# Weighing the values in float32r parts in the first layer's attention, and a beat of three steps for one kind of head

## The chip, the cores and the metric

The kernel runs on one core of a Trainium2 chip. The metric is the device time of one execution in microseconds (us), taken as the median of several runs of one kernel. A profiled execution gives the trace; its own time stands beside its span below.

TensorE is called PE in the profile (PEld: its loads of the stationary operand), VectorE DVE, ScalarE ACT, GpSimd POOL, SyncE SP.

## The reference

A decoder trunk of two layers over 256 positions and 2048 channels. The first layer's attention has two kinds of heads; this case is about the product of softmax weights and values in both.

```python
def even_mixer(x, w_in, sinks, w_out):
    h = jnp.einsum('bsd,de->bse', x, w_in)
    # kind A: 16 query heads on 2 key/value heads, window 128, a learned sink per head, ALiBi
    oa, _ = banded_attention(qa, ka, va, A_WINDOW - 1, 1, ...)
    # kind B: 8 heads, three dilations (1, 4, 16), merged by their denominators
    for gi, (window, dil) in enumerate(B_PATTERNS):
        o, lse = banded_attention(to_strided(qb, dil), to_strided(kb, dil), to_strided(vb, dil), ...)
    mix = jax.nn.softmax(jnp.stack(lses), axis=0)
    ...
    return jnp.einsum('bse,ed->bsd', y, w_out)      # y: A's 16 heads, then B's 8

def reference(x, ...):
    for layer in range(DEPTH):
        x = layer_norm(ALPHA * x + mixer(x), ...)
        x = layer_norm(ALPHA * x + sqrelu_mlp(x, ...), ...)
```

All is float32. The second layer has other mixers, and the code of their attention stays as it is.

## The kernel before, in words

**Dense products.** All weights come from memory once, in units of 512 KB (128 partitions of 1024 floats). SP's queue loads a unit into a `raw` tile; ACT casts it to float32r (`w_hi`, line 120); DVE subtracts and keeps the rest, also as float32r (`w_lo`, line 121). A dense product is hi times hi, lo times hi and hi times lo, each one pass of the array in float32r. `ws` (lines 329 and 332) has the weights as the stationary operand and streams x (512 columns with both parts of x, 256 with its high part); `as_` (lines 379 to 381) has x or y as the stationary operand and streams the weights, 512 columns at a time. Splits run three units ahead of PE, loads five.

**Attention.** It is cut into steps that are laid between the units of the dense work: after each unit the loop calls `pump`, and that calls `attn_step` once. The order is fixed by the program; each engine works through its own queue in that order. A `Job` holds one kind of heads, taken in pairs. A started pair computes scores (`qk`, line 699, float32), bias and maxima on DVE, exponentials on ACT one or two steps on, the division on DVE after that. `lag` steps later each head's weights are turned by three PE transposes into the one PSUM tile `pt`, and ACT copies them to an SBUF tile `pT` (`flip`, lines 260 and 262), one flip a step. Two steps after the flip of the odd head of a pair, `weigh` multiplies the pair's `pT` with the values. Jobs: A has 16 heads and starts a pair every second step (`pace=2`); B0 and B1 have 4 heads with three dilations each (`per=3`), which add up in one PSUM tile `o`.

In `weigh` the values are stationary, 128 keys by 64 columns, so the two heads of a pair stand side by side in the array; the `pT` stream is 256 columns for the first block of keys and 128 for the second, all in float32 (lines 279 and 281), which PE runs as two instructions for each product. After the last one ACT casts `o` to a float32r `y` and DVE subtracts its rest (lines 285 and 286).

So there are 8 weighings for A and 12 for B, 20 in all. The last of B1 come in `finish`, without dense work between the steps: the third column block of the output projection calls it when it needs B1's result, two units before its end.

**The names used below.** W is one weighing, F one flip's three transposes, S the scores of one pair (two heads). The tile pools are rings: `S` 4, `pT` 4, `qk` 15, `xfull` 2, `o` 1, `pt` 1, `sc` 2, `acc` 4.

Of the kernel before, what the change touches and what calls it, by code (L numbers as in the profile page):

```python
# [30 lines left out]
HD = 64  # L31
# [35 lines left out]
class Stream:  # L67


    def __init__(self, k):  # L70
        self.k = k
        self.units = []
        self.nd = 0
        self.ns = 0
        self.nu = 0
        self.live = {}
# [74 lines left out]
class Job:  # L151


    def __init__(self, name, n, per, score, stages, value, lag, y, pace=2):
        self.name, self.n, self.per, self.lag, self.pace = name, n, per, lag, pace
        self.score, self.stages, self.value, self.y = score, stages, value, y
        self.left = n // 2
        self.out = []
        self.s = {}
        self.pt = {}  # L160
        self.o = None


class Trunk:
# [48 lines left out]
    def attn_step(self):  # L213
        i = self.i
        self.i += 1
        if self.flips and self.flips[0][0] <= i:
            _, job, h, u = self.flips.popleft()
            self.at_step(i, 2, self.flip, job, h, u)
            if h % 2:
                self.at_step(i + 2, 1, self.weigh, job, (h - 1, h), u)  # L220
        for _, _, fn, args in sorted(self.due.pop(i, []), key=lambda t: t[:2]):
            fn(*args)
        if not self.todo or i < self.turn:
            return
        job, h, u = self.todo[0]
        per, pair = job.per, (h, h + 1)
        if h not in job.s:
            need = 2 if per > 1 else 1
            if self.s_live + need > self.s_bufs:
                return  # L230
            self.s_live += need
            if per > 1:
                for g in pair:
                    job.s[g] = self.at.tile([P, per * 384], F32, name="S", bufs=self.s_bufs)
            else:
                both = self.at.tile([P, 768], F32, name="S", bufs=self.s_bufs)
# [17 lines left out]
    def flip(self, job, h, u):  # L254

        nc = self.nc
        st = job.s[h]
        pt = self.ps.tile([P, 384], F32, name="pt")
        for b in range(3):
            nc.tensor.transpose(pt[:, b * P:(b + 1) * P], st[:, u * 384 + b * P:u * 384 + (b + 1) * P], self.ident)  # L260
        pT = self.at.tile([P, 384], F32, name="pT", bufs=self.pt_bufs)
        nc.scalar.copy(pT, pt)
        job.pt[(h, u)] = pT
        if u == job.per - 1 and (job.per > 1 or h % 2):
            self.s_live -= 1

    def weigh(self, job, heads, u):
        nc = self.nc
        first, last = u == 0, u == job.per - 1
        if first and heads[0] % 2 == 0:  # L270
            job.o = self.ps.tile([P, S], F32, name="o")
        o = job.o
        for blk in range(2):
            for h in heads:
                rows = slice((h % 2) * HD, (h % 2) * HD + HD)
                w = job.pt[(h, u)]
                v = job.value(h, u, blk)
                if blk == 0:
                    nc.tensor.matmul(o[rows, :], v, w[:, 0:S], start=first, stop=False, skip_group_check=True)  # L279
                else:  # L280
                    nc.tensor.matmul(o[rows, P:S], v, w[:, S:S + P], start=False, stop=last, skip_group_check=True)
        if last and heads[-1] % 2:
            y = job.y(len(job.out))
            yh, yl, _ = y
            nc.scalar.copy(yh, o)
            nc.vector.tensor_tensor(yl, o, yh.bitcast(F32), op=ALU.subtract)
            job.out.append(y)
            job.left -= 1

    def y_at(self, k=None):  # L290
        return self.parts(self.at.tile([P, 2 * S], F32R, name="y", bufs=self.y_bufs))

    def parts(self, t):
        return t[:, 0:S], t[:, S:2 * S], t
# [149 lines left out]
    def setup(self):  # L444
        nc, a, const = self.nc, self.a, self.const
        nc.scalar.preload_act_table_set("natural_log_exp_and_others")
        zeros = self.at.tile([P, 512], BF16, name="zeros")
        nc.vector.memset(zeros, 0.0)
        self.keep_clock(IDLE[0], zeros)
        self.ident = const.tile([P, P], F32, name="ident")  # L450
        nc.sync.dma_start(self.ident, a["ident"])
        self.x = self.res.tile([P, 2, D], F32, name="x_res")
        xv = a["x"][0].rearrange("(t p) d -> p t d", p=P)
        for c0, c1, ahead in ((0, 256, 1), (256, 512, 2), (512, 1024, 4), (1024, 1536, 5), (1536, 2048, 6)):
            nc.sync.dma_start(self.x[:, :, c0:c1], xv[:, :, c0:c1])
            self.w._dma(ahead)
        gb = self.at.tile([16, 8, P], F32, name="gb")
        rg = self.at.tile([6, P], F32, name="rg")
        self.sinks = const.tile([P, 16], F32, name="sinks")
        self.masks = self.at.tile([P, 4, 384], F32, name="masks")  # L460
        small = [(gb[:, i * 2:i * 2 + 2, :], a[nm].rearrange("l (k p) -> k l p", p=P))
                 for i, nm in enumerate(("ln1_g", "ln1_b", "ln2_g", "ln2_b"))]
        small += [(rg[0:4, :], a["odd_q_norm_g"][0].rearrange("(k p) -> k p", p=P)),
                  (rg[4:6, :], a["odd_kv_norm_g"][0].rearrange("(k p) -> k p", p=P)),
                  (self.masks, a["m_even"]), (self.sinks, a["even_sinks"][0].unsqueeze(0).to_broadcast([P, 16]))]

        def load(some):
            for dst, src in some:
                nc.gpsimd.dma_start(dst, src)

# [276 lines left out]
    def even(self):  # L747
        nc = self.nc
        slopes = alibi(16)
        qa = self.project(512, scale=0.125) + self.project(512, scale=0.125)  # L750
        kd = self.tile2()
        va = self.tile2()
        kvf = self.at.tile([P, 2, S], F32, name="kvf", bufs=1)
        vf = kvf[:, 1, :]

        def take(f, bank):
# [10 lines left out]
        def flip_v():  # L767
            pt = self.ps.tile([P, 384], F32, name="pt")
            for t in range(2):
                nc.tensor.transpose(pt[:, t * P:(t + 1) * P], vf[:, t * P:(t + 1) * P], self.ident)  # L770
            nc.vector.tensor_copy(va[:, :, 0:P], pt[:, 0:S].rearrange("p (t c) -> p t c", t=2))

        self.at_step(self.i, 0, flip_v)
        top, power, divide = self.softmax(1, sink=lambda h: self.sinks[:, h:h + 1])
# [6 lines left out]
            nc.vector.scalar_tensor_tensor(st, self.masks[:, 0, :], -slopes[h], sc, op0=ALU.mult, op1=ALU.add)  # L781
            top(h, st)

        def value(h, u, blk):
            return va[:, blk, (h // 8) * HD:(h // 8) * HD + HD]

        self.vb = []
        ja = Job("A", 16, 1, score, (bias, power, divide), value, 5, self.y_at)
        self.queue(ja)
        jb = [self.even_b(0, self.y_at), self.even_b(1, self.x_slot)]  # L790
        self.finish(jb[0])
# [10 lines left out]
        for c in range(3):  # L802
            o = self.as_(late if c == 2 else ys, 12 if c == 2 else 10, 512)
            self.add_res(o, c, True, st if c == 2 else None)
            self.pump()
        for c in range(2):
            o = self.as_(jb[1].out, 2, 512)
# [4 lines left out]
    def even_b(self, half, y):  # L812
        nc = self.nc
        sl = alibi(8)
        qkv = []
# [9 lines left out]
            if u == 2:  # L825
                top(h, st)

        def value(h, u, blk):
            return qkv[u][2][:, blk, h * HD:h * HD + HD]

        job = Job(f"B{half}", 4, 3, score, (bias, power, divide), value, 4, y)
        for gi in range(3):
            q = self.project(256, scale=0.125)[0]
            k = self.project(256)[0]
# [296 lines left out]
    def go(self):  # L1131
        tc = self.tc
        self.plan()
        for layer in range(2):
            if layer == 0:
                self.s_bufs, self.pt_bufs, self.qk_bufs, self.y_bufs = 4, 4, {"qk": 15}, 10
            else:
                self.s_bufs, self.pt_bufs, self.qk_bufs, self.y_bufs = 4, 4, {"c": 8, "d": 10}, 14
            with tc.tile_pool(name=f"at{layer}", bufs=1) as self.at:
# [44 lines left out]
```

## Time and profile before

| | |
|---|---|
| median of 3 runs | 2182.63 us (2182.18 to 2182.82) |
| profiled execution, own time | 2183.56 us |
| its span | 2181.8 us |
| PE busy / DVE busy / ACT busy | 2161.2 / 1392.9 / 1063.9 us |
| granted TensorE clock | 0.999 |
| first layer's attention in the span | about 85 to 370 us |
| 85 to 135 us: DVE busy, ACT busy | 44.77, 35.09 of 50 us |

How to read it: the share of busy time says that PE is nearly always at work, but matmuls are pipelined and their ends are modelled, so what one piece of work is worth is read from the distance of ends in the chain of work that ended last. The chain's rows are "start, length, what"; a piece ends where the next begins. In the timelines and groups a row's length is that of the whole instruction, which overlaps its neighbours.

### The profile page before, as it was taken

What the parts mean: (1) busy time and instruction counts of PE and PEld (TensorE: products, weight loads), DVE (VectorE), ACT (ScalarE), POOL (GpSimd) and SP (SyncE); (2) the same over time, 40 slices, a digit from 0 to 9 for tenths busy, and PEclk for the clock granted to TensorE, in tenths of its full rate; (3) what the DMA queues carried; (4) which work ended last, traced back from release to release, by engine and by line L of the source; (5) the groups of instructions that cost most, each with busy time, mean ns of one, the idle gap of its engine ahead of it and who ended that gap; (6) DMA issues with size and microseconds to landing.
All of it is one profiled execution on the core that took longest, in us unless ns stands there. A gap on an engine that the chain in (4) does not pass through costs nothing.

```text
span 2181.8 us, 29446 instructions
## 1 busy us (share of the span) xinstructions
PE 2161.2 (99%) x11324; PEld 1816.7 (83%) x11324; DVE 1392.9 (64%) x1912; ACT 1063.9 (49%) x1532; POOL 34.4 (2%) x64
## 2 busy tenths in 40 slices
PE   9999999999999999999999999999999999999998
PEld 7878887888888888888878787778888888888886
DVE  5765566775465556456568888878645655554656
ACT  4554544554354355345345667545534534543542
POOL 0000000000000000000012000000000000000000
PEclk9999999999999999999999999999999999999999
DMA  7545554565656665656558554466665656556553
GB/s 265 157 136 174 158 166 149 189 201 193 192 180 203 193 188 190 194 175 205 190 155 210 167 150 145 155 193 204 206 193 179 198 197 192 185 194 192 186 197 119
DMA packets 222269, 399.02 MB, mean 183 GB/s; under 512 B 12778, under 2 KB 52416, under 8 KB 221360
## 3 DMA queue, kind: packets, MB, share of 16 engines
q1 hardware_dynamic: 219424, 386.78, 56.2%
q0 software_dynamic: 2416, 9.84, 1.9%
q8 instruction: 88, 1.44, 0.3%
q10 hardware_dynamic: 288, 0.52, 0.1%
q14 instruction: 53, 0.43, 0.1%
HBM read 395.00 MB, written 2.10 MB: 182 GB/s over the span
## 4 chain that ended last, share of the span: by engine, by line
PE 94%; issue 2%; DMA 1%; DVE 1%; ACT 1%; POOL 1%; SPq 0%; POOLq 0%; ACTq 0%; DVEq 0%
PE acc L332 18%; PE acc L379 15%; PE acc L380 15%; PE acc L381 15%; PE acc L329 9%; PE sc L332 5%; PE sc L329 3%; PE pt L332 3%; PE o L332 3%; PE sc L699 2%; PE o L329 1%; PE pt L329 1%; PE pt L260 1%; PE o L279 1%; PE acc L985 1%
## 5 line engine op out<-in xcount | busy, mean ns | idle before, releaser
L121 DVE TENSOR_TENSOR w_lo<-raw,w_hi 128x1024 fp32r<-128x1024 f32 (+3 forms) x748 | 883.6, 1197 | 605.2 <-ACT w_hi L120 601.2
L120 ACT CAST w_hi<-raw 128x1024 fp32r<-128x1024 f32 (+3 forms) x748 | 760.3, 1030 | 733.1 <-PE acc L381 440.2
L332 PE MATMUL acc<-x,w_hi 128*128 128x512 f32 x1824 | 453.7, 394 | 4.3 <-DVE x L520 4.1
L379 PE MATMUL acc<-w_hi,h_hi 128*128 128x512 f32 x1016 | 395.3, 389 | 0.0
L380 PE MATMUL acc<-w_lo,h_hi 128*128 128x512 f32 x1016 | 395.3, 389 | 0.0
L381 PE MATMUL acc<-w_hi,h_lo 128*128 128x512 f32 x1016 | 395.2, 389 | 0.0
L332 PEld LDWEIGHTS acc<-x,w_hi 128*128 128x128 f32 x1824 | 330.9, 189 | 68.1 <-issue 2.9
L329 PEld LDWEIGHTS acc<-x,w_lo 128*128 128x128 f32 x1824 | 244.1, 191 | 17.9 <-issue 3.8
L329 PE MATMUL acc<-x,w_lo 128*128 128x256 f32 x1824 | 254.4, 284 | 0.0
L381 PEld LDWEIGHTS acc<-w_hi,h_lo 128*128 128x128 f32 x1016 | 190.7, 188 | 39.6
L379 PEld LDWEIGHTS acc<-w_hi,h_hi 128*128 128x128 f32 x1016 | 190.7, 188 | 39.4
L380 PEld LDWEIGHTS acc<-w_lo,h_hi 128*128 128x128 f32 x1016 | 190.7, 188 | 39.3
L332 PE MATMUL sc<-x,w_hi 128*128 128x512 f32 x512 | 138.7, 392 | 0.0
L379 PE MATMUL acc<-w_hi,x 128*128 128x512 f32 (+1 forms) x304 | 119.5, 393 | 0.3 <-DVE x L519 0.2
L381 PE MATMUL acc<-w_hi,x 128*128 128x512 f32 (+1 forms) x304 | 115.8, 381 | 0.0
L380 PE MATMUL acc<-w_lo,x 128*128 128x512 f32 (+1 forms) x304 | 115.7, 381 | 0.0
L345 ACT ACTIVATE xfull<-acc 128x256 f32<-128x256 f32 x130 | 49.5, 383 | 128.5 <-PE acc L332 77.6
L332 PEld LDWEIGHTS sc<-x,w_hi 128*128 128x128 f32 x512 | 91.0, 189 | 14.6
L329 PE MATMUL sc<-x,w_lo 128*128 128x256 f32 x512 | 84.3, 282 | 0.0
L329 PEld LDWEIGHTS sc<-x,w_lo 128*128 128x128 f32 x512 | 76.6, 190 | 6.4
L332 PE MATMUL pt<-x,w_hi 128*128 128x512 f32 x256 | 79.3, 391 | 0.0
L332 PE MATMUL o<-x,w_hi 128*128 128x512 f32 x256 | 78.9, 389 | 0.0
(208 smaller groups left out, 1954.5 us busy)
## 6 DMA issues: line engine op xcount, KB each, us to landing
raw<-in_mlp_w SPq DMA_DIRECT2D x512, 512.0 KB, 4.1
raw<-in_even_w_in SPq DMA_DIRECT2D x92, 512.0 KB, 4.1
raw<-in_odd_w_in SPq DMA_DIRECT2D x56, 512.0 KB, 4.5
raw<-in_odd_w_out SPq DMA_DIRECT2D x32, 512.0 KB, 3.7
raw<-in_even_w_out SPq DMA_DIRECT2D x24, 512.0 KB, 3.9
gb_rows<-in_ln_g POOLq DMA_DIRECT2D x3, 1024.0 KB, 5.1
gb_rows<-in_ln_b POOLq DMA_DIRECT2D x3, 1024.0 KB, 7.1
raw<-in_odd_w_uq SPq DMA_DIRECT2D x8, 384.0 KB, 4.7
```

What stands on the lines that cost most here:

```text
L120: nc.scalar.copy(h, r)
L121: nc.vector.tensor_tensor(l, r, h.bitcast(F32), op=ALU.subtract)
L260: nc.tensor.transpose(pt[:, b * P:(b + 1) * P], st[:, u * 384 + b * P:u * 384 + (b + 1) * P], self.ident)
L279: nc.tensor.matmul(o[rows, :], v, w[:, 0:S], start=first, stop=False, skip_group_check=True)
L329: nc.tensor.matmul(banks[f][:, S:2 * S], lo[:, c:c + P], xs[kt + kk][0], start=False, stop=wide and kt + kk == nkt - 1, skip_group_check=True)
L332: nc.tensor.matmul(banks[f], hi[:, c:c + P], xs[kt + kk][2], start=kt + kk == 0, stop=not wide and kt + kk == nkt - 1, skip_group_check=True)
L345: nc.scalar.activation(t, bank[:, S:2 * S], AF.Copy, scale=scale)
L379: nc.tensor.matmul(outs[t], xh[:, ts], hi[:, c:c + width], start=first, stop=False, skip_group_check=True)
L380: nc.tensor.matmul(outs[t], xh[:, ts], lo[:, c:c + width], start=False, stop=False, skip_group_check=True)
L381: nc.tensor.matmul(outs[t], xl[:, ts], hi[:, c:c + width], start=False, stop=last, skip_group_check=True)
L699: nc.tensor.matmul(sc[:, cols], q[:, qs], k[:, ks], start=True, stop=True, skip_group_check=True)
L985: nc.tensor.matmul(banks[h], hi[:, c:c + P], both, start=k == 0, stop=False, skip_group_check=True)
```

## The change

For both kinds of heads in the first layer, the weighing is done with float32r parts.

- `flip` makes two tiles: ACT casts `pt` to a float32r `pT`, then DVE subtracts and writes the rest to `pL`. Both read the PSUM tile `pt`. `pT` and `pL` have three buffers each (before: `pT` four).
- The values are split as well (`split_values`): for each key block and head 128 columns hold the high part (64) and the low part (64). A does this once (`va`); B does it for every pair and dilation one step before the weighing (`value_parts`, tile `vp`, two buffers), by an ACT cast and a DVE subtraction.
- `weigh_parts`: for each head and key block the 128 columns are stationary, and `pT`, then `pL` are streamed: 8 matmuls for a pair, four of 256 columns and four of 128. The two heads have a column range of `o` each (now 512 columns). The output rows of high and low values lie in the two halves of the partitions; after the last matmul two ACT copies and two DVE additions bring them together in an `xfull` tile, and the cast and the subtraction to `y` follow from there.
- A starts a pair every third step (`pace=3`).
- For room: `zeros` uses a buffer of `pT`, the gains (`gb`, `rg`) use a buffer of `S`, `kvf` comes from the `qk` ring, and `va` has a shape of its own in it.

```diff
@@ attn_step
-                self.at_step(i + 2, 1, self.weigh, job, (h - 1, h), u)
+                if job.parts:
+                    self.at_step(i + 1, 4, self.value_parts, job, h - 1, u)
+                self.at_step(i + 2, 1, self.weigh_parts if job.parts else self.weigh, job, (h - 1, h), u)
@@ flip
+            hi = self.at.tile([P, 384], F32R, name="pT", bufs=self.pt_bufs)
+            lo = self.at.tile([P, 384], F32R, name="pL", bufs=self.pt_bufs)
+            nc.scalar.copy(hi, pt)
+            nc.vector.tensor_tensor(lo, pt, hi.bitcast(F32), op=ALU.subtract)
+            job.pt[(h, u)] = hi, lo
@@ new
+    def split_values(self, dst, src):
+        self.nc.scalar.copy(dst[:, :, :, 0, :], src)
+        self.nc.vector.tensor_tensor(dst[:, :, :, 1, :], src, dst[:, :, :, 0, :].bitcast(F32), op=ALU.subtract)
+
+    def weigh_parts(self, job, heads, u):
...
+        for j, h in enumerate(heads):
+            for blk, cols, ws in ((0, slice(j * S, j * S + S), slice(0, S)), (1, slice(j * S + P, j * S + S), slice(S, S + P))):
+                stat = v(j, blk)
+                for n, w in enumerate(job.pt[(h, u)]):
+                    nc.tensor.matmul(o[:, cols], stat, w[:, ws], start=first and j + blk + n == 0,
+                                     stop=last and blk == 1 and n == 1, skip_group_check=True)
...
+        nc.scalar.copy(other[lo], o[hi, 0:S])
+        nc.scalar.copy(other[hi], o[lo, S:2 * S])
+        nc.vector.tensor_tensor(full[lo], o[lo, 0:S], other[lo], op=ALU.add)
+        nc.vector.tensor_tensor(full[hi], o[hi, S:2 * S], other[hi], op=ALU.add)
...
+        nc.scalar.copy(yh, full)
+        nc.vector.tensor_tensor(yl, full, yh.bitcast(F32), op=ALU.subtract)
@@ even
-        ja = Job("A", 16, 1, score, (bias, power, divide), value, 5, self.y_at)
+        ja = Job("A", 16, 1, score, (bias, power, divide), None, 5, self.y_at, pace=3, parts=parts)
@@ even_b
+        def parts(h, u):
+            v = self.at.tile([P, 2, 2, 2, HD], F32R, name="vp", bufs=2)
+            self.split_values(v, qkv[u][2][:, :, h * HD:(h + 2) * HD].rearrange("p t (h e) -> p t h e", h=2))
+            return lambda j, blk: v[:, blk, j].rearrange("p a e -> p (a e)")
-        job = Job(f"B{half}", 4, 3, score, (bias, power, divide), value, 4, y)
+        job = Job(f"B{half}", 4, 3, score, (bias, power, divide), None, 4, y, parts=parts)
@@ go
-                self.s_bufs, self.pt_bufs, self.qk_bufs, self.y_bufs = 4, 4, {"qk": 15}, 10
+                self.s_bufs, self.pt_bufs, self.qk_bufs, self.y_bufs = 4, 3, {"qk": 15}, 10
```

**How the order moves.** PE, a pair of A during an `as_` product: `acc` rows are dense work, `o` is W, `pt` F, `sc` S. Before:

```order
L279 MATMUL o<-pT,qk 64x256 x2
L281 MATMUL o<-pT,qk 64x128 x2
L260 MATMUL pt<-ident,S 128x128 x3
L699 MATMUL sc<-qk 128x128 x2
L699 MATMUL sc<-qk 128x256 x2
L379 MATMUL acc<-w_hi,x_143 128x512
L380 MATMUL acc<-w_lo,x_143 128x512
```

The same place in the changed kernel (`pL` is the low part of the weights; `qk` is here `va`):

```order
L322 MATMUL o<-pT,qk 128x256
L322 MATMUL o<-pL,qk 128x256
L322 MATMUL o<-pT,qk 128x128
L322 MATMUL o<-pL,qk 128x128
L322 MATMUL o<-pT,qk 128x256
L322 MATMUL o<-pL,qk 128x256
L322 MATMUL o<-pT,qk 128x128
L322 MATMUL o<-pL,qk 128x128
L264 MATMUL pt<-ident,S 128x128 x3
L429 MATMUL acc<-w_hi,x_142 128x512
L430 MATMUL acc<-w_lo,x_142 128x512
```

W has eight rows of its own, and S no longer stands right behind W and F: it comes a unit later, behind the pair's other flip.

DVE at the same place, from one pair's `y` on. Before (`dn`, `rc` and `S<-S,rc` are a head's division, `S<-masks,sc` with `mx` and `nm` a head's bias and maximum):

```order
L286 TENSOR_TENSOR y<-o,y 128x256
L735 TENSOR_TENSOR dn<-dn,es 128x2
L737 RECIPROCAL rc<-dn 128x2
L739 TENSOR_SCALAR S<-S,rc 128x128
L739 TENSOR_SCALAR S<-S,rc 128x256
L781 SCALAR_TENSOR_TENSOR S<-masks,sc 128x384
L713 TENSOR_REDUCE mx<-S 128x1 x2
L716 TENSOR_SCALAR nm<-mx,sinks 128x2
L781 SCALAR_TENSOR_TENSOR S<-masks,sc 128x384
```

Now:

```order
L331 TENSOR_TENSOR xfull<-o,xfull 64x256
L332 TENSOR_TENSOR xfull<-o,xfull 64x256
L336 TENSOR_TENSOR y<-xfull,y 128x256
L269 TENSOR_TENSOR pL<-pt,pT 128x384
L785 TENSOR_TENSOR dn<-dn,es 128x2
L787 RECIPROCAL rc<-dn 128x2
L789 TENSOR_SCALAR S<-S,rc 128x128
L789 TENSOR_SCALAR S<-S,rc 128x256
L121 TENSOR_TENSOR w_lo<-raw,w_hi 128x1024
L269 TENSOR_TENSOR pL<-pt,pT 128x384
```

Two additions and a `pL` are new behind the weighing, and the second flip's `pL` stands behind a weight split (`w_lo`); a pair has three steps, so three `w_lo` in place of two.

PE at the end of B1, where no dense work lies between the steps. Before:

```order
L260 MATMUL pt_3463<-ident_88,S_2716 128x128 x3
L260 MATMUL pt_3475<-ident_88,S_2715 128x128 x3
L279 MATMUL o_3458<-pT_3438,vb_1923 64x256
L279 MATMUL o_3458<-pT_3467,vb_1923 64x256
L281 MATMUL o_3458<-pT_3438,vb_1923 64x128
L281 MATMUL o_3458<-pT_3467,vb_1923 64x128
L260 MATMUL pt_3485<-ident_88,S_2716 128x128 x3
L279 MATMUL o_3458<-pT_3479,vb_2351 64x256
```

Now (the values come from `vp`):

```order
L264 MATMUL pt_3694<-ident_88,S_2896 128x128 x3
L264 MATMUL pt_3708<-ident_88,S_2895 128x128 x3
L322 MATMUL o_3685<-pT_3660,vp_3716 128x256
L322 MATMUL o_3685<-pL_3661,vp_3716 128x256
L322 MATMUL o_3685<-pT_3660,vp_3716 128x128
L322 MATMUL o_3685<-pL_3661,vp_3716 128x128
L322 MATMUL o_3685<-pT_3698,vp_3716 128x256
L322 MATMUL o_3685<-pL_3699,vp_3716 128x256
L322 MATMUL o_3685<-pT_3698,vp_3716 128x128
L322 MATMUL o_3685<-pL_3699,vp_3716 128x128
L264 MATMUL pt_3727<-ident_88,S_2896 128x128 x3
L322 MATMUL o_3685<-pT_3712,vp_3735 128x256
```

The sequence of F and W is the same. DVE in that stretch, before:

```order
L121 TENSOR_TENSOR w_lo_3417<-raw_3280,w_hi_3416 128x1024
L121 TENSOR_TENSOR w_lo_3441<-raw_3309,w_hi_3440 128x1024
L121 TENSOR_TENSOR w_lo_3470<-raw_3333,w_hi_3469 128x1024
L286 TENSOR_TENSOR x0_3407<-o_3458,x0_3407 128x256
L121 TENSOR_TENSOR w_lo_3510<-raw_3365,w_hi_3509 128x1024
```

Now:

```order
L269 TENSOR_TENSOR pL_3699<-pt_3694,pT_3698 128x384
L121 TENSOR_TENSOR w_lo_3703<-raw_3533,w_hi_3702 128x1024
L269 TENSOR_TENSOR pL_3713<-pt_3708,pT_3712 128x384
L307 TENSOR_TENSOR vp_3716<-vb_2019,vp_3716 128x4x64
L269 TENSOR_TENSOR pL_3732<-pt_3727,pT_3731 128x384
L307 TENSOR_TENSOR vp_3735<-vb_2464,vp_3735 128x4x64
L331 TENSOR_TENSOR xfull_3746<-o_3685,xfull_3746 64x256
```

DVE had no part in the chain from flip to weighing; now every flip has a subtraction there, and each weighing's `vp` is written after the flip that stands just ahead of it.

More of the change, by code (lines that the diff above doesn't have):

```diff
@@ L151, with __init__ @@
 class Job:
-    def __init__(self, name, n, per, score, stages, value, lag, y, pace=2):
+    def __init__(self, name, n, per, score, stages, value, lag, y, pace=2, parts=None):
         self.name, self.n, self.per, self.lag, self.pace = name, n, per, lag, pace
         self.score, self.stages, self.value, self.y = score, stages, value, y
+        self.parts = parts
+        self.v = {}
         self.left = n // 2
@@ L260, in flip @@
             nc.tensor.transpose(pt[:, b * P:(b + 1) * P], st[:, u * 384 + b * P:u * 384 + (b + 1) * P], self.ident)
-        pT = self.at.tile([P, 384], F32, name="pT", bufs=self.pt_bufs)
-        nc.scalar.copy(pT, pt)
-        job.pt[(h, u)] = pT
+        if job.parts:
+            hi = self.at.tile([P, 384], F32R, name="pT", bufs=self.pt_bufs)
[3 more added lines that the diff above has]
+            job.pt[(h, u)] = hi, lo
+        else:
+            pT = self.at.tile([P, 384], F32, name="pT", bufs=self.pt_bufs)
+            nc.scalar.copy(pT, pt)
+            job.pt[(h, u)] = pT
         if u == job.per - 1 and (job.per > 1 or h % 2):
@@ L288, in weigh, with value_parts @@
             job.left -= 1
+    def value_parts(self, job, h, u):
+        job.v[(h, u)] = job.parts(h, u)
+    def split_values(self, dst, src):
+        self.nc.scalar.copy(dst[:, :, :, 0, :], src)
+        self.nc.vector.tensor_tensor(dst[:, :, :, 1, :], src, dst[:, :, :, 0, :].bitcast(F32), op=ALU.subtract)
+    def weigh_parts(self, job, heads, u):
+        nc = self.nc
+        first, last = u == 0, u == job.per - 1
+        if first:
+            job.o = self.ps.tile([P, 2 * S], F32, name="o")
+        o = job.o
+        v = job.v.pop((heads[0], u))
+        for j, h in enumerate(heads):
[4 more added lines that the diff above has]
+                                     stop=last and blk == 1 and n == 1, skip_group_check=True)
+        if not last:
+            return
+        t = self.small.tile([P, 2, S], F32, name="xfull", bufs=2)
+        other, full = t[:, 0, :], t[:, 1, :]
+        lo, hi = slice(0, HD), slice(HD, P)
+        nc.scalar.copy(other[lo], o[hi, 0:S])
+        nc.scalar.copy(other[hi], o[lo, S:2 * S])
+        nc.vector.tensor_tensor(full[lo], o[lo, 0:S], other[lo], op=ALU.add)
+        nc.vector.tensor_tensor(full[hi], o[hi, S:2 * S], other[hi], op=ALU.add)
+        y = job.y(len(job.out))
+        yh, yl, _ = y
+        nc.scalar.copy(yh, full)
+        nc.vector.tensor_tensor(yl, full, yh.bitcast(F32), op=ALU.subtract)
+        job.out.append(y)
+        job.left -= 1
     def y_at(self, k=None):
@@ L446, in setup @@
         nc.scalar.preload_act_table_set("natural_log_exp_and_others")
-        zeros = self.at.tile([P, 512], BF16, name="zeros")
+        zeros = self.at.tile([P, 512], BF16, name="pT", bufs=self.pt_bufs)
         nc.vector.memset(zeros, 0.0)
@@ L456, in setup @@
             self.w._dma(ahead)
-        gb = self.at.tile([16, 8, P], F32, name="gb")
-        rg = self.at.tile([6, P], F32, name="rg")
+        gains = self.at.tile([16, 9, P], F32, name="S", bufs=self.s_bufs)
+        gb, rg = gains[:, 0:8, :], gains[0:6, 8, :]
         self.sinks = const.tile([P, 16], F32, name="sinks")
@@ L751, in even @@
         kd = self.tile2()
-        va = self.tile2()
-        kvf = self.at.tile([P, 2, S], F32, name="kvf", bufs=1)
+        va = self.at.tile([P, 2, 2, 2, HD], F32R, name="qk", bufs=self.qk_bufs["qk"])
+        kvf = self.tile2()
         vf = kvf[:, 1, :]
@@ L770, in flip_v @@
                 nc.tensor.transpose(pt[:, t * P:(t + 1) * P], vf[:, t * P:(t + 1) * P], self.ident)
-            nc.vector.tensor_copy(va[:, :, 0:P], pt[:, 0:S].rearrange("p (t c) -> p t c", t=2))
+            self.split_values(va, pt[:, 0:S].rearrange("p (t h e) -> p t h e", t=2, h=2))
         self.at_step(self.i, 0, flip_v)
@@ L782, in bias @@
             top(h, st)
-        def value(h, u, blk):
-            return va[:, blk, (h // 8) * HD:(h // 8) * HD + HD]
+        def parts(h, u):
+            return lambda j, blk: va[:, blk, h // 8].rearrange("p a e -> p (a e)")
         self.vb = []
-        ja = Job("A", 16, 1, score, (bias, power, divide), value, 5, self.y_at)
+        ja = Job("A", 16, 1, score, (bias, power, divide), None, 5, self.y_at, pace=3, parts=parts)
         self.queue(ja)
@@ L826, in bias, with parts @@
                 top(h, st)
-        def value(h, u, blk):
-            return qkv[u][2][:, blk, h * HD:h * HD + HD]
-        job = Job(f"B{half}", 4, 3, score, (bias, power, divide), value, 4, y)
+        def parts(h, u):
+            v = self.at.tile([P, 2, 2, 2, HD], F32R, name="vp", bufs=2)
+            self.split_values(v, qkv[u][2][:, :, h * HD:(h + 2) * HD].rearrange("p t (h e) -> p t h e", h=2))
+            return lambda j, blk: v[:, blk, j].rearrange("p a e -> p (a e)")
+        job = Job(f"B{half}", 4, 3, score, (bias, power, divide), None, 4, y, parts=parts)
         for gi in range(3):
```

## The prediction

> **What bounds the kernel now.** I read the page first, then PE's waits up to 400 us and the stretch in which kind A runs, in busy us of 50.
>
> ```profile
> PE 2161.2 (99%) x11324; PEld 1816.7 (83%) x11324; DVE 1392.9 (64%) x1912; ACT 1063.9 (49%) x1532; POOL 34.4 (2%) x64
> PE pt L260 <- ACT pT L262: 0.6, 1, 0.6
> 85.00:135.00 50.00, 50.00 (x291) 38.56 (x290) 44.77 (x124) 35.09 (x102) 0.00 (x0) 1.00 0.45 131
> ```
>
> PE's queue is the time: a microsecond taken from PE here is a microsecond of the end, and so is one that PE waits. In the whole attention it waits once, 0.6 us, for a `pT` copy. But DVE is at 90% while A runs (44.77 of 50), so work moved to DVE there isn't free by itself.
>
> What one weighing W costs now I read from the chain, where each piece's length is the distance of ends. First W, F and S in one group, then F and S without W, then (B) W and F, and F alone:
>
> ```profile
> 103.02 0.58 PE o L279 x4
> 103.60 0.22 PE o L281 x4
> 103.82 0.48 PE pt L260 x3
> 104.30 0.86 PE sc L699 x8
> 105.16 0.43 PE acc L379
> ...
> 95.77 0.33 PE pt L260 x3
> 96.10 0.85 PE sc L699 x8
> 96.95 0.67 PE acc L329 x4
> ...
> 234.33 0.58 PE o L279 x4
> 234.91 0.22 PE o L281 x4
> 235.13 0.48 PE pt L260 x3
> 235.61 1.85 PE acc L332 x8
> 237.46 0.95 PE acc L329 x8
> 238.41 0.33 PE pt L260 x3
> ...
> 239.69 1.84 PE acc L332 x8
> ```
>
> Dense matmuls come every 0.23 (eight of 512 columns in 1.84) or 0.119 (eight of 256 in 0.95); the first behind S costs 0.20 more (0.43; four in 0.67). So the first group is 0.58+0.22+0.48+0.86+0.20 = 2.34 and the second 0.33+0.85+0.20 = 1.38: W is worth 0.96. In B, 0.58+0.22+0.48+0.01 = 1.29 against 0.33: 0.96 again. Of that 0.80 is W itself, the rest makes F dearer behind it (0.48 for 0.33).
>
> **The change part by part: W.** The new W is four float32r matmuls of 256 columns and four of 128, each with its own load of 128 stationary columns. The 256-column one costs 0.119. The 128-column one has no row. Two rows bound the load, for 64 and for 128 stationary columns:
>
> ```profile
> L281 PEld LDWEIGHTS o<-pT,qk x56: 137/137/137, 103.2 to 271.5; 128*64 128x64 f32 x56
> L332 PEld LDWEIGHTS o<-x,w_hi x256: 187/188/188, 426.4 to 2083.3; 128*128 128x128 f32 x128
> ```
>
> 64 more columns take 51 ns more, so 128 occupy the load path for about 0.10, which covers a whole 128-column matmul if that streams at the rate of the others (half of 0.119). F's transposes, 128 columns with 128 stationary ones, run at 0.33/3 = 0.11. I take 0.11, the nearest row: W = 4 x 0.119 + 4 x 0.11 = 0.92. Lower end: half a 256-column slot, 0.06, W = 0.71. Upper end: the float32 rate, where one 128-column product costs 0.22 (row L281 x4: two heads side by side), W = 1.36. Because no mode changes between dense work and W, F behind it is 0.33. So W saves 0.04 (from +0.25 to -0.40), for 17 of the 20 weighings 0.7 us (from 4.2 saved to 6.8 lost); the last three follow by themselves.
>
> The Trainium skill, page "TensorE: Matmul & The Clock Gate", section "LDWEIGHTS (loading the stationary operand)", gives a load as its columns over 1.2 per ns, an estimate of 107 ns for 128 columns; the two rows agree with it, and it speaks against this change, since eight such loads alone are 0.86. The same page's "Back-to-back issue gap" gives an isolated matmul N/2.4 + 2.5 ns, by which W would be an estimate of 0.66 and the weighings 5 us cheaper; the 256-column row is at 119 ns and not at its 109.
>
> **The end of B1.** Three weighings stand here without dense work between them, and PE already waits for the copies:
>
> ```profile
> 360.84 0.58 PE o L279 x4
> 361.64 0.49 PE pt L260 x3
> 362.21 0.49 ACT pT L262
> 362.75 0.55 PE pt L260 x3
> 366.10 0.43 PE acc L379
> ...
> 362.59 1.05 ACT L120 CAST w_hi<-raw 128x1024 fp32r<-128x1024 f32 x1
> 363.67 1.23 DVE L121 TENSOR_TENSOR w_lo<-raw,w_hi 128x1024 fp32r<-128x1024 f32 x1 [2.83 <-ACT w_hi L120]
> ```
>
> Now `pt` is free only after DVE's `pL`, and W waits for `vp`. With DVE prices from the next fence (`pL` and bias are both 128x384: 0.55; the `vp` parts are as large as `y`: 0.37 on ACT, 0.42 on DVE) I walk it. W from 360.84 to 361.76, F to 362.09, `pT` to 362.64, `pL` to 363.20. F again, 363.25 to 363.79 (before: 363.29). ACT must end the cast of a weight unit (362.54 to 363.59), then `pT` to 364.34 and the `vp` cast to 364.61. DVE has a `w_lo` ahead, 363.62 to 364.76, then `pL` to 365.3, `vp` to 365.67. W waits for that: first matmul 0.05 + 0.39 after it, seven more 0.80, end 366.9. F to 367.24, `pT` 367.8, `pL` 368.35, `vp` 368.7, last W ends 369.9. Before, W ended at 366.10 and the next matmul lost 0.20 more: **+3.6 us** (2.5 if DVE and ACT overlap better at each of the two turns, 4.5 if another split gets in between). What is late next, the two copies, two additions and `y` (about 2.3 us), is covered: 18 matmuls of 0.23 = 4.1 us follow before their first reader.
>
> **Kind A, DVE.** The prices of its loop (DVE's rows, then ACT's; a row's spacing counts):
>
> ```profile
> 112.47 0.42 DVE L286 TENSOR_TENSOR y<-o,y 128x256 fp32r<-128x256 f32 x1 [0.20 <-ACT y L285]
> 112.81 0.15 DVE L735 TENSOR_TENSOR dn<-dn,es 128x2 f32<-128x2 f32 x1
> 113.67 0.55 DVE L781 SCALAR_TENSOR_TENSOR S<-masks,sc 128x384 f32<-128x384 f32 x1
> 115.03 0.55 DVE L781 SCALAR_TENSOR_TENSOR S<-masks,sc 128x384 f32<-128x384 f32 x1
> 116.40 1.22 DVE L121 TENSOR_TENSOR w_lo<-raw,w_hi 128x1024 fp32r<-128x1024 f32 x1
> 117.53 0.15 DVE L735 TENSOR_TENSOR dn<-dn,es 128x2 f32<-128x2 f32 x1
> ...
> 112.07 0.37 ACT L285 CAST y<-o 128x256 fp32r<-128x256 f32 x1 [1.05 <-PE o L281]
> 112.59 0.48 ACT L262 COPY pT<-pt 128x384 f32<-128x384 f32 x1 [0.15 <-PE pt L260]
> 112.97 0.40 ACT L725 ACTIVATE S<-S,nm 128x128 f32<-128x128 f32 x1
> 114.05 1.04 ACT L120 CAST w_hi<-raw 128x1024 fp32r<-128x1024 f32 x1
> ```
>
> Bias with maximum 1.36, division 0.86, `w_lo` 1.13, `y` 0.34, exponentials 1.08. One pair in the new order, from the first addition: two additions 0.75; then ACT in its order, `y` 0.40, `pT` 0.38, exponentials 1.08, cast 1.04; then DVE, whose queue stands behind the `w_lo` that waits for that cast: `w_lo` 1.13, `pL` 0.50, division 0.86, two biases 2.72, two `w_lo` 2.26. Sum 11.1 us. PE needs for the same pair three units (36 matmuls of 0.23 = 8.28), W 0.92, F 0.33, F and S 1.38: 10.9 us. So DVE loses 0.2 a pair where `as_` runs (four pairs), and about 0.6 where `ws` runs (three), whose joins add some 0.5 a pair (two ACT copies, two DVE additions as large as `y` every four units): 2.6 us. PE feels it when the first `pL` of a pair ends after the second F should start, since both use `pt`: it ends 2.13 after the first addition begins and F comes 2.6 after, so 0.5 to 0.6 us are free. I take **+2.0 us**, between 0 (DVE and ACT overlap a little better) and 3.5 (the four copies at an `as_` end delay ACT too).
>
> **At nothing.** `pace=3` moves F and S of A to other units and leaves their number; B0's first scores come eight steps later and the rest of B0 stands as before. In the rest of B a step has 0.33 + 2.76 between flips, and `pT`, `pL` and one cast need 0.1+0.38+0.55 before `pt` is free; `vp` is written about 1.5 after the flip and read 2.8 after. If a `w_lo` of 1.13 got ahead of it at each of nine such weighings, up to 1 us each would be exposed; I see no such order. The setup's renamed buffers are read long before their next use, and no load on SP's or POOL's queue changes its place.
>
> **Sum.** -0.7 + 3.6 + 2.0 = +4.9 us: 2183.56, the profiled execution's time, becomes 2188.5. The median of the runs shown is 0.93 lower, so 2187.5.
>
> **Rivals.**
> 1. The 128-column matmul in float32r is no faster than float32. For it: no such form stands in the trace, the narrowest has 256. Against: nothing, only the rows' common rate. W is 1.36: +6.8, the end of B1 3 x 0.44 longer (+4.9), and A's PE period is 11.3, longer than DVE's 11.1, so no wait there. +11.7: 2194.3.
> 2. Not slower: the load hides behind the stream and W is 0.71. For it: dense matmuls of 512 columns hide their loads. Against: the two PEld rows. -4.2, the end of B1 +3.0, A's PE period shorter by 0.2, so the wait there +3.0: +1.8, 2184.4. It turns to faster where A's loop closes without waits: -1.2, 2181.4; and it decides from a 128-column slot under 0.08.
> 3. Forecast without DVE's loop in A (DVE's slack is enough): +2.9, 2185.5. For it: 90% busy before without one wait. Against: a second `pL` behind a `w_lo` that waits for a cast is new.
>
> **How the numbers follow.** A time within 0.2% (4.4 us) is about what a measurement of this kernel can't tell from no change; the upper line is at 2187.0. My forecast has a chance of 0.42 (2186 to 2189.5, two thirds above the line: 0.28), rival 3 0.19 (0.02 above), rival 1 0.25 (all above), rival 2 0.14 (0.04 faster than the line, 0.10 within). Slower 0.55, same 0.41, faster 0.04. The range reaches from rival 2 without most of its wait (2183) to rival 1 (2194.5).
>
> **What would show it.** PE group `o` with 160 matmuls in place of 160 instructions at 64 columns, and a chain row of about 0.92 for eight of them: 0.7 or 1.4 would prove rival 2 or 1. PE waiting for `pL` before `pt` in A, eight times some 0.3 us, and none under rival 3. Around 362 to 370 us, PE waits for `vp` and `pL` of 1 to 2 us each, and W's end some 3.6 us later against the W at 360.84. I would be wrong above all if W's narrow matmuls have another price, or if ACT and DVE close the loop in A sooner.

## The result and the profile after

The changed kernel takes 2197.37 us (median of six runs, 2196.87 to 2198.63) against 2182.94 (six runs of the kernel before on the same chip, 2182.18 to 2183.18): ratio 1.0067, interval 1.0057 to 1.0076. It is 14.4 us slower. 2187.5 was forecast, with a range to 2194.5.

First PE's waits of the changed kernel up to 420 us (in total, times, longest), then PE, PEld, DVE, ACT and POOL busy and the granted clock in the two stretches around B1's flips, after and (second fence) before.

```profile
PE pt L264 <- DVE pL L269: 5.8, 7, 2.0
PE o L322 <- DVE vp L307: 3.4, 2, 1.9
330.00:350.00 20.00, 17.98 (x82) 14.55 (x81) 16.92 (x29) 10.08 (x18) 0.00 (x0) 0.91 0.51 158
350.00:385.00 35.00, 30.34 (x152) 25.10 (x151) 19.03 (x30) 14.28 (x26) 0.00 (x0) 0.90 0.36 106
```

```profile
330.00:350.00 20.00, 20.00 (x106) 15.63 (x105) 14.72 (x21) 10.48 (x17) 0.00 (x0) 1.00 0.59 184
350.00:385.00 35.00, 34.33 (x173) 26.41 (x172) 20.93 (x25) 13.64 (x18) 0.00 (x0) 1.00 0.43 127
```

In this attention PE now waits 9.2 us for DVE where it waited 0.6 us for a copy, and its clock, 1.00 before, averages 0.91 and 0.90 there. Waits and clock are two separate losses.

To place them I took from the traces the start of every dense matmul and summed the distance from one to the next, grouped by what stands between the two (the number of distances is in the heading). The distances run from 69 to 370 us of the kernel before; A is what lies before 226 us there, B what lies behind. A kernel with A at `pace=3` in float32 (the third experiment) stands in for A before, since the change regroups the steps.

| us in sum | A: second flip and S (9) | A: W and F (7) | B: F alone (12) | B: W and F (8) | end of B1 (1) | B: dense next to dense (572) |
|---|---|---|---|---|---|---|
| float32 | 13.12 | 9.75 | 5.27 | 11.17 | 5.58 | 113.95 |
| changed | 16.69 | 9.39 | 9.15 | 11.17 | 10.59 | 116.26 |
| difference | +3.57 | -0.36 | +3.88 | 0 | +5.01 | +2.31 |

These sum to 14.4. The whole of both stretches grew from 300.70 to 315.12 us, by 14.42, as much as the medians. Nothing is lost later. The 0 for W and F in B hides two things: seven of the eight cost 0.05 less, and one in B0 costs 1.78 for 1.42; `vp` a step earlier (below) brings that one to 1.37.

**W.** Its length in the chain, and the end of B1 in the same chain:

```profile
368.27 0.87 PE o L322 x8
369.14 0.37 PE pt L264 x3
...
369.96 1.06 ACT w_hi L120
371.02 0.02 issue
371.04 1.23 DVE w_lo L121
372.27 0.47 DVE pL L269
372.74 0.34 DVE vp L307
373.08 0.04 issue
373.12 1.43 PE o L322 x8
374.55 0.67 PE pt L264 x3
...
375.76 0.56 DVE pL L269
376.31 0.34 DVE vp L307
376.66 0.04 issue
376.70 1.97 PE o L322 x8
378.67 0.53 PE acc L429
```

The first W takes 0.87, by the chain of ends; the two after it, with the same eight matmuls, 1.43 and 1.97. They run at a falling clock after waits of 1.86 and 1.49 us. In steady state W with its flip costs 1.371 between dense matmuls where float32 costs 1.424: the change is worth 0.05 us for each weighing.

**B1's first flips.** PE's timeline (start, length, what, and in brackets the idle time before it), then DVE's ahead of the subtraction that PE waits for:

```profile
336.25 0.39 PE L431 MATMUL acc<-w_hi,y 128*128 128x512 f32 x1
338.67 0.55 PE L264 MATMUL pt<-ident,S 128*128 128x128 f32 x3 [2.02 <-DVE pL L269]
...
340.25 0.63 PE L430 MATMUL acc<-w_lo,y 128*128 128x512 f32 x1
340.67 0.63 PE L431 MATMUL acc<-w_hi,y 128*128 128x512 f32 x1
```

```profile
331.82 1.41 DVE L763 TENSOR_REDUCE mx<-S 128x1 f32<-128x384 f32 x2
...
333.35 1.23 DVE L121 TENSOR_TENSOR w_lo<-raw,w_hi 128x1024 fp32r<-128x1024 f32 x1
...
334.68 1.14 DVE L789 TENSOR_SCALAR S<-S,rc 128x384 f32<-128x384 f32 x2
335.74 1.21 DVE L121 TENSOR_TENSOR w_lo<-raw,w_hi 128x1024 fp32r<-128x1024 f32 x1
336.86 1.28 DVE L612 SCALAR_TENSOR_TENSOR x_res<-x_res,acc 128x512 f32<-128x512 f32 x2
338.06 0.55 DVE L269 TENSOR_TENSOR pL<-pt,pT 128x384 fp32r<-128x384 f32 x1
```

DVE has no gap here: maxima, splits, divisions and a residual stand ahead of the first `pL`, and the second F, which needs the one tile `pt`, waits 2.02 us. Behind it the dense matmuls of 512 columns come every 0.43 us (340.25 to 340.67) and not every 0.23. DVE's queue was as full at this place in the kernel before:

```profile
333.36 1.28 DVE L562 SCALAR_TENSOR_TENSOR x_res<-x_res,acc 128x512 f32<-128x512 f32 x2
334.55 0.16 DVE L737 RECIPROCAL rc<-dn 128x2 f32<-128x2 f32 x1
334.75 1.14 DVE L739 TENSOR_SCALAR S<-S,rc 128x384 f32<-128x384 f32 x2
```

### The profile page after: what moved, and what is told of

Read it like the earlier page. It is cut to its first block, busy times and chain, and to the rows that moved or that the text cites. A ratio compares the mean times of both kernels' runs of the same rounds, so it can differ in the third digit from the quotient of the medians.

```text
span 2195.1 us, 29533 instructions
## 1 busy us (share of the span) xinstructions
PE 2164.1 (99%) x11323; PEld 1826.5 (83%) x11324; DVE 1427.8 (65%) x1988; ACT 1075.8 (49%) x1569; POOL 34.4 (2%) x64
## 4 chain that ended last, share of the span: by engine, by line
PE 89%; DVE 4%; issue 3%; ACT 2%; DMA 2%; POOL 1%; SPq 0%; POOLq 0%; ACTq 0%; DVEq 0%
PE acc L382 17%; PE acc L429 14%; PE acc L430 14%; PE acc L431 14%; PE acc L379 9%; PE sc L382 5%; PE sc L379 3%; PE pt L382 3%; PE o L382 3%; PE o L379 1%; PE pt L379 1%; PE sc L749 1%; DVE w_lo L121 1%; PE pt L264 1%; DMA raw<-in_even_w_in 1%
```

## The experiments

The table's columns serve as the measure below; each time has beside it its ratio to the kernel before, with the interval.

**One part at a time.** A alone in parts (first line pair: B's `Job` gets `value` again), B alone in parts (second pair), and the kernel before with only the beat of A changed (third).

```diff
-        job = Job(f"B{half}", 4, 3, score, (bias, power, divide), None, 4, y, parts=parts)
+        job = Job(f"B{half}", 4, 3, score, (bias, power, divide), value, 4, y)
...
-        ja = Job("A", 16, 1, score, (bias, power, divide), None, 5, self.y_at, pace=3, parts=parts)
+        ja = Job("A", 16, 1, score, (bias, power, divide), value, 5, self.y_at)
...
-        ja = Job("A", 16, 1, score, (bias, power, divide), value, 5, self.y_at)
+        ja = Job("A", 16, 1, score, (bias, power, divide), value, 5, self.y_at, pace=3)
```

> Kind A weighed in parts every third step, kind B as before. Theory (the loss is made at a few places where PE waits for DVE, since the flip's PSUM tile and the values' parts hang on DVE): only A's share stays, the +3.1 us that the trace of the changed kernel shows between 85 and 188 us: 2186; the clock stays full throughout. Rival (each weighing in parts costs more, wherever it stands): 8 of 20 weighings, 5.8 of 14.4 us: 2188.7.

> Kind B weighed in parts, kind A in float32 every second step as before. Theory: the waits at the first flips of B0 and B1, the end of B1 and the halved clock behind them stay, about 11 us: 2194. Rival (cost per weighing): 12 of 20, 8.6 us: 2191.6.

> The kernel before with nothing but the beat of three steps for A. Theory: F and S move to other units, nothing waits: 2183, within 0.5 us. Rival (the beat itself pushes work into worse places): +2 to +3 us.

A alone: 2186.38 us (1.0014, 1.0005 to 1.0024). B alone: 2194.52 (1.0050, 1.0035 to 1.0065). The beat alone: 2182.84 (1.0000, 0.9990 to 1.0009). Each median is near its theory's. So A costs 3.4, B 11.5 and the beat nothing, 14.9 for 14.4. That the sum is so near is partly chance: over the whole of both stretches the profiled execution with A alone lost 3.2 us and that with B alone 9.6, where the changed kernel lost 14.4. With B alone the clock stayed at 1.00 at 340 us, and 2.4 us were lost in the second layer instead (told at the end).

**The beat of A.** `pace` 2 and 4 instead of 3.

```diff
-        ja = Job("A", 16, 1, score, (bias, power, divide), None, 5, self.y_at, pace=3, parts=parts)
+        ja = Job("A", 16, 1, score, (bias, power, divide), None, 5, self.y_at, pace=4, parts=parts)
```

> The changed kernel with A at a pair every second step. Theory: DVE needs about 10 us a pair and PE 8.1, so PE waits some 1.5 to 2 us for each of six or seven pairs: 10 us over the changed kernel, 2207. Rival (the beat of three is what costs in A): 2 to 3 us under it, 2194.5.

> The changed kernel with A at a pair every fourth step. Theory (in A a round trip through ACT's and DVE's queues, about 11 us a pair, is longer than PE's three units with W, F and S; with four units PE needs 13.7 and the round trip some 12.2): no wait for pL between 85 and 220 us, 3 us less than the changed kernel: 2194.3. Rival (the waits hang on the order inside the queues, at any beat): within 1 us of the changed kernel.

Two steps: 2200.08 us (1.0077, 1.0062 to 1.0092), 2.7 above the changed kernel and not the 10 that DVE's sum of work gave. Four steps: 2196.48 (1.0060, 1.0046 to 1.0074), 0.9 under the changed kernel, which is the rival's. With four steps the trace names three waits in A, 0.5 us in all, yet six of A's second flips take 0.68 to 0.85 between dense matmuls instead of 0.477, together 1.9 us. The rows of PE overlap, so part of a wait that short leaves no gap to be named; the distance of starts shows it.

**`vp` a step earlier.**

```diff
-                    self.at_step(i + 1, 4, self.value_parts, job, h - 1, u)
+                    self.at_step(i, 4, self.value_parts, job, h - 1, u)
```

> The changed kernel with B's values split one step earlier, right behind the flip of the pair's odd head. Theory (at the end of B1 the weighings wait for vp, which stands behind a later flip's copy and subtraction): 2 to 2.5 us less, 2195. Rival (the chain of flips sets the end of B1, vp only ends last by chance): within 0.5 us of the changed kernel.

2193.76 us (1.0048, 1.0033 to 1.0063): 3.6 less, more than the 2 to 2.5 expected. In the columns of the profiled execution the end of B1 fell from 10.59 to 9.37 and W with F in B from 11.17 to 10.76: 1.6 us of waiting for `vp`, as the theory had it. Dense next to dense fell from 116.26 to 115.00, because the clock stayed up around 340 us:

```profile
330.00:350.00 20.00, 17.98 (x91) 14.70 (x90) 17.77 (x30) 10.84 (x21) 0.00 (x0) 1.00 0.50 158
```

PE's busy time is the same 17.98 as in the changed kernel and the wait ahead of B1's second flip is 2.02 us again (2.708 between dense matmuls, 2.713 there), but the clock is 1.00 and not 0.91. The same wait lowers it in one execution and not in another, so this 1.3 us can't be put down to the edit.

**Keeping PE at work while it waits.** 47 bf16 matmuls of 256 columns, whose result nobody reads, stand where PE waits at B1's second flip and at its end.

```diff
+        n = {("B1", 1, 0): 16, ("B1", 2, 2): 10}.get((job.name, h, u), 0)
+        if n:
+            self.warm(n)
...
+        n = {("B1", 2, 1): 12, ("B1", 2, 2): 9}.get((job.name, heads[0], u), 0)
+        if n:
+            self.warm(n)
```

> The changed kernel with 47 idle matmuls of 256 columns in bf16 (about 0.11 us each) laid where PE waits: 16 before the second flip of B1, 12, 10 and 9 at its last weighings and flip; no reader uses them. Theory (the halved clock comes from PE's idle time): the granted clock stays at 1.00 from 330 to 385 us, and 1.4 us at 340 and 2 us at 375 are saved: 2194. Rival (the clock falls for another reason than idle time): it falls again, 2197.4 or up to 1 us more.

2194.86 us (1.0051, 1.0034 to 1.0068). Clock and columns answer:

```profile
330.00:350.00 20.00, 19.74 (x106) 16.16 (x105) 17.37 (x29) 10.56 (x20) 0.00 (x0) 1.00 0.48 158
350.00:385.00 35.00, 33.72 (x192) 28.08 (x191) 22.27 (x34) 15.79 (x27) 0.00 (x0) 1.00 0.39 121
```

Dense next to dense is 113.68, as low as in float32, and the end of B1 9.20 for 10.59. So 2.3 + 1.4 = 3.7 of the 14.4 us were the clock, and the waits at the end of B1 alone cost 9.20 - 5.58 = 3.6. In the medians 2.5 show; the profiled execution lost 2.4 again at 1215 us, in the second layer, which is told at the end.

That PE's idle time is the cause is shown for the end of B1: every profiled kernel with B1 in parts has waits there and, without these matmuls, a clock of 0.80 to 0.95 from 350 to 385 us. For the place at 340 us it isn't shown by this run alone. Seven profiled kernels have the same wait of 2.02 us there without these matmuls; the clock fell to 0.91 in three (changed, two steps, four steps) and stayed at 1.00 in four (B alone, `vp` early, and the two with B in parts and the joining late, below).

**B one step later** (`lag` 5 instead of 4), and **a mixture**: A at `pace` 4, B0 in parts with `lag` 5, B1 in float32.

```diff
-        job = Job(f"B{half}", 4, 3, score, (bias, power, divide), None, 4, y, parts=parts)
+        job = Job(f"B{half}", 4, 3, score, (bias, power, divide), None, 5, y, parts=parts)
...
+        job = Job(f"B{half}", 4, 3, score, (bias, power, divide), value, 4 if half else 5, y,
+                  parts=None if half else parts)
```

> The changed kernel with B's flips one step later (lag 5 for 4), so that DVE has one unit's time more to end the pair's bias, maxima and division before the first subtraction. Theory (the first flips of B0 and B1 meet a DVE that is behind): the waits of 0.8 and 2.0 us there go, and with the latter the halved clock; the end of B1 gets one step more without dense work, about 1 us: 2194. Rival (the first subtraction waits at any lag, since DVE stays behind): 2197 or more.

> A in parts every fourth step, B0 in parts with lag 5, B1 in float32 as before. Theory (a weighing in parts is 0.09 us cheaper on PE, 0.87 for 0.96; all loss was made by waits): no wait is left beside those of the kernel before, 14 weighings give 1.2 us: 2181.8, 0.05% under the kernel before. Rival (cost per weighing): 14 of 20, 2193; a rival between: some waits in B0 stay, 2184.

The first: 2198.30 us (1.0067, 1.0054 to 1.0081), the rival's. Flips alone fell only to 8.39, and B1's second flip still takes 2.38 between dense matmuls: one step later DVE's next division and split stand ahead of `pL`, which starts at 340.07. The end of B1 now holds one more step without dense work: 14.33, at a clock of 0.80 from 350 to 385 us. The mixture: 2186.05 (1.0014, 1.0005 to 1.0023), 4 us above the theory and 2 above the rival between: A keeps the hidden waits of the four-step beat, and B0's flips still lose 1.1 (1.175 and 0.765 for 0.476 and 0.366).

**Who holds `pt`?** F needs `pt`, which the changed kernel frees after DVE's subtraction. Four kernels: in one ACT makes a second copy (into a part of `S` that is no longer used) and DVE reads that; the next is the same with `vp` earlier; in the other two DVE reads only SBUF, so that ACT's one copy frees `pt`, with every instruction in its place (`pL` is then zero, and the low weights' part is left out of the result), without and with the earlier `vp`.

```diff
+            full = st[:, u * 384:u * 384 + 384]
...
+            nc.scalar.copy(full, pt)
-            nc.vector.tensor_tensor(lo, pt, hi.bitcast(F32), op=ALU.subtract)
+            nc.vector.tensor_tensor(lo, full, hi.bitcast(F32), op=ALU.subtract)
```

```diff
-            nc.vector.tensor_tensor(lo, pt, hi.bitcast(F32), op=ALU.subtract)
+            nc.vector.tensor_tensor(lo, hi.bitcast(F32), hi.bitcast(F32), op=ALU.subtract)
```

> The changed kernel, but ACT copies the flip's PSUM tile a second time into the dead place of the softmax weights in SBUF, and DVE subtracts from that copy: DVE no longer stands between a flip and the next one, its work stays the same, ACT has 0.4 us more a flip. Theory (the loss is DVE's place in the PSUM tile's chain): the waits in A (3 us), at the first flips of B0 and B1 (3.3 us) and the halved clock behind the latter (1.4 us) go, the end of B1 stays: 2190. Rival (DVE and ACT are short of time, whatever waits for them): the waits move to the weighings and to the weights' parts, gain under 2 us: 2196.

> Both edits, the second copy by ACT and the values split a step earlier. Theory: all three places are mended but for ACT's and DVE's bare chain at the end of B1 (some 3 us), the clock stays full: 2187. Rival (short of time): 2193 or more.

> The changed kernel, but the low part of the weights is taken from the SBUF copy alone (copy minus copy, so the low weights are zero and that part of the product is left out of the result; every instruction stays, on its engine and in its place). So pt is free as soon as ACT has copied it, as in the kernel before, while DVE's queue and ACT's queue hold the same work. Theory: what A and the first flips of B lose is the time that pt is held by DVE's subtraction. Then PE has hardly a wait of F for DVE, A's share of the loss falls from about 3.1 us to 0.5 or less, the first flips of B0 and B1 from 4 to under 1 us, and the end of B1, where W also waits for vp, keeps 2 to 4 us. Sum 2186 to 2189 us. Rival: the queues of ACT and DVE are too long, whoever holds pt; then W waits for pL and vp where F waited, and the time is within 3 us of the changed kernel's 2197.4.

> As the run with pt held by ACT's copy alone (low weights zero, that part left out of the result), and with vp written a step earlier, as in the run that gained 3.6 us by that. Theory: no copy or subtraction on DVE stands between a flip and the next any more, and the values lie ready, so what is left is W's own saving (20 times 0.09 = 1.8 us) against what the end of B1 still waits for the last pL: 2182 to 2185 us, at most 1 us faster than the kernel before. Rival: ACT's and DVE's queues still hold W; 2190 or more.

| | time, us | ratio | A: second flip and S | B: F alone | B: W and F | end of B1 |
|---|---|---|---|---|---|---|
| changed | 2197.37 | 1.0057 to 1.0076 | 16.69 | 9.15 | 11.17 | 10.59 |
| second copy | 2201.33 | 1.0068 to 1.0098 | 19.16 | 5.30 | 14.79 | 11.90 |
| the same, `vp` early | 2194.94 | 1.0038 to 1.0068 | 19.14 | 5.30 | 11.24 | 8.82 |
| DVE reads SBUF | 2196.77 | 1.0047 to 1.0077 | 16.26 | 5.29 | 14.42 | 11.14 |
| the same, `vp` early | 2188.51 | 1.0012 to 1.0031 | 16.32 | 5.29 | 11.24 | 7.33 |

By their times the first, second and third of these four lie on the rival's side or beyond it, and the last between. For B the theory holds halfway. Flips alone are back at float32's 5.27, so there the subtraction did hold `pt`. But without the earlier `vp` the lost time stands at the next W, since DVE's backlog is the same; PE's waits of the fourth row:

```profile
PE o L322 <- DVE vp L307: 6.8, 5, 2.5
PE pt L264 <- ACT pT L268: 2.7, 6, 1.0
```

Both together, 2188.51, take away 8.9 us. In A the theory fell: the second flips keep 16.3 us although DVE doesn't hold `pt`, and with two copies on ACT they take 19.2. What PE waits for in the fourth row is ACT's copy, and ACT's timeline in that kernel shows why it is late, with DVE's beside it:

```profile
148.39 0.37 ACT L330 COPY xfull<-o 64x256 f32<-64x256 f32 x1
150.23 0.40 ACT L335 CAST y<-xfull 128x256 fp32r<-128x256 f32 x1 [1.47 <-DVE xfull L332]
150.54 0.47 ACT L268 CAST pT<-pt 128x384 fp32r<-128x384 f32 x1
```

```profile
147.06 2.36 DVE L121 TENSOR_TENSOR w_lo<-raw,w_hi 128x1024 fp32r<-128x1024 f32 x2 [0.16 <-ACT w_hi L120]
149.34 0.41 DVE L331 TENSOR_TENSOR xfull<-o,xfull 64x256 f32<-64x256 f32 x1
149.76 0.43 DVE L332 TENSOR_TENSOR xfull<-o,xfull 64x256 f32<-64x256 f32 x1
```

F's transposes ended near 147.3. ACT could have copied `pt` at 148.8, but the cast to `y` stands ahead of it and waits 1.47 us for DVE's two additions, and those stand behind two `w_lo`.

**The joining behind the flip.** So the joining (two copies, two additions, cast and subtraction to `y`) was laid behind the flip of its step: in the changed kernel, with `vp` early, and with A alone in parts.

```diff
                 self.at_step(i + 2, 1, self.weigh_parts if job.parts else self.weigh, job, (h - 1, h), u)
+                if job.parts:
+                    self.at_step(i + 2, 2.5, self.join_parts, job, u)
```

> The changed kernel, with the joining of a weighing (two ACT copies, two additions, the cast and the subtraction to y) laid behind the flip of the same step instead of ahead of it. In the changed kernel and in the run with pt freed by ACT alone, ACT's copy of pt stands behind the cast to y, and that cast waits 1.5 us for DVE's additions, which stand behind two w_lo. Theory: this queue, and not the hold of pt by the subtraction, is what the second flip of each pair in A waits for. The stretch between two dense matmuls that holds the second flip and the scores falls from a mean of 1.85 to 1.5 us, in nine places about 3.3 us in all; B's first flips and the end of B1 stay. 2193.5 to 2194.5 us. Rival: DVE's queue alone (pL behind the w_lo) holds the second flip: not under 2196.

> The late joining together with vp written a step earlier. Theory: the two gains are in different places and add: 3.3 and 3.6 us below the changed kernel, 2190 to 2191 us. What is left are B's first flips behind DVE's backlog and the last flips of B1. Rival: with ACT's and DVE's orders moved in both, new waits take half of it: 2192.5 or more.

> Only A in parts, with the late joining; B as before in float32. Theory: no wait is left in A, and W saves 0.05 us for each of eight weighings: 2182.6 to 2183.2 us, no difference from the kernel before. Rival: A still loses by DVE's load, 2185 or more.

2196.56 us (1.0060, 1.0046 to 1.0074); with `vp` early 2192.54 (1.0043, 1.0029 to 1.0057); A alone 2184.76 (1.0008, 0.9998 to 1.0017). The first two lie on the rival's side and the third between. The columns say how much of the theory holds: A's second flips went from 16.69 to 15.00, half of the loss. By place, in the run with A alone: five of the seven that follow the first two are at float32's 1.507, and two keep 1.94 and 2.81 (1.40 and 1.51 in float32). Those two stand in `ws`. DVE's timeline at the second of them, and PE's behind it, in the run with A alone:

```profile
146.74 2.36 DVE L121 TENSOR_TENSOR w_lo<-raw,w_hi 128x1024 fp32r<-128x1024 f32 x2 [0.16 <-ACT w_hi L120]
149.02 0.55 DVE L271 TENSOR_TENSOR pL<-pt,pT 128x384 fp32r<-128x384 f32 x1
```

```profile
149.62 0.55 PE L266 MATMUL pt<-ident,S 128*128 128x128 f32 x3 [1.08 <-DVE pL L271]
```

Half of A's loss was the joining's place ahead of the flip, where ACT's copy stood behind the cast and DVE's `pL` behind the additions; no run parts these two. The other half is DVE's own, two splits ahead of `pL`; it is read from the timeline, and no run took those splits away. A's column gained 1.7 us here and the medians 0.8. One reason is a new wait: with the joining late, one weighing in B0 takes 2.66 between dense matmuls for 1.78. The spread of these four runs, 2195.1 to 2197.4, doesn't settle the rest.

No version is faster than the kernel before. There was little to win: 0.05 us times 20 weighings is 1 us, 0.05% of the time.

## Why the prediction was wrong

- **W** (forecast 0.92, W with F 0.04 less than in float32): right. It is 0.87, and 0.05 less. That is near the estimate worked out from the Trainium skill, page "TensorE: Matmul & The Clock Gate", section "LDWEIGHTS (loading the stationary operand)": eight loads are 0.86. Rival 1 (1.36) and rival 2 (0.71) are out. The sum held and not each price: in one W of B1 (346.48 to 347.35) the narrow matmuls start 0.06 to 0.11 ahead of the next, where 0.11 was put, and the wide ones 0.11 to 0.17, where it was 0.119.
- **The beat at nothing**: right, 2182.84.
- **A's loop, +2.0, bounds 0 to 3.5**: mis-sized. The second flips lost 3.57, and A alone 3.4. The sum of DVE's work for a pair was no measure: the step failed in "one pair in the new order", which let ACT go on to `pT` right after `y`, while `y` waits for additions behind one or two splits. Taking the joining out of the flip's way brought back half of the loss. The working had a place for the two additions, but started the clock at the first of them, and not at the splits that they stand behind.
- **End of B1, +3.6, bounds 2.5 to 4.5**: the walk through the queues was right, 3.6 at full clock. It came to 5.0 because W took 1.43 and 1.97 at the fallen clock. The walk didn't price that.
- **"In the rest of B ... at nothing"**: the step that failed most. It walked a flip in steady state and looked for a `w_lo` ahead of `vp`. The exposed places are the first flips of B0 and B1, where DVE is behind with maxima, divisions and splits, by more than one step of `lag` makes good. The kernel before had that backlog without effect, since DVE had no part between flips; with `pt` freed by ACT's copy the flips are back at 5.29. +3.88, of it 2.24 at B1's second flip, 1.04 at B0's, and 0.3 at each of two later ones.
- **The clock**: missing. It took 2.3 us of dense matmuls and 1.4 of the end of B1, 3.7 in all in the profiled execution; some 1.8 of it (0.09 of 20 us) fell at 340 us, where the same wait had no such effect in other executions. Without it the loss would have been 10.7, still twice the forecast.

In the forecast's terms: -0.7 for W came true, but for one wait in B0; 3.6 came true and got 1.4 more; 2.0 was 3.6; two terms that stood at nothing, 3.9 and 2.3, make up most of the rest.

## What to carry to other kernels

When an engine enters a chain that it had no part in (here DVE between flip and flip), look in the trace of before for the places where that engine has no gap, and price the first use there, not the steady state. A queue is also late by what its own waiting instruction waits for: the copy was held by a cast that it doesn't depend on. Bound the gain first: a saving of 0.05 us in 20 places can't pay for one exposed wait of 2 us.

## What the runs showed of the hardware

A wait of about 2 us can halve TensorE's clock for some 3.5 us (0.09 of 20 us at half rate is 3.6), but not each time: a wait of 2.02 us did in the changed kernel, and the same 2.02 with `vp` early didn't. The Trainium skill, page "TensorE: Matmul & The Clock Gate", section "What's actually happening", tells of a free-running window of about 3.4 us that must be idle; the length of the slow stretch agrees, and the wait that sets it off is shorter here.

The same happens in code that the change doesn't touch. One wait in the second layer, in the kernel before and in that with idle matmuls:

```profile
1205.38 0.50 PE L985 MATMUL acc<-y,w_hi 128*128 128x512 f32 x1 [1.31 <-DVE c L346]
```

```profile
1215.69 0.50 PE L1049 MATMUL acc<-y,w_hi 128*128 128x512 f32 x1 [2.11 <-DVE c L408]
...
1215.00:1220.00 5.00, 4.31 (x15) 3.72 (x16) 4.09 (x8) 2.59 (x4) 0.00 (x0) 0.66 0.51 140
```

At 1.31 us the clock stayed at 1.00; at 2.11 it fell to 0.66 over 5 us. With B alone in parts it was the same (2.14 us, 0.66), in the changed kernel 1.17 us and no fall. Against the changed kernel it cost the execution with idle matmuls 2.4 us, 0.9 by the wait and 1.5 by the clock. Why the wait is longer in some executions is open. So a difference of 1 to 2 us between two medians of this kernel needs the places before it means anything.
